# A decoder layer with 32 experts on one core: how the first expert is gathered and multiplied, where the selection stands, and the last output chunk in halves

## The chip, the core and the metric

The kernel runs on one core of one Trainium2 chip. The metric is device time in microseconds, the median of the runs; lower is better. The core has five engines with a queue each, worked off in order: TensorE (PE; its weight loads are shown apart, as PEld), VectorE (DVE), ScalarE (ACT), GpSimd (POOL) and SyncE (SP), which here does nothing but issue transfers.

## What is computed

One layer for 256 tokens of width 2048, all in float32:

```
h = rms_norm(x); proj = h @ w_in                     # 2048 x 6144
mixed = concat(moba_attention(...), diff_attention(...))
x = x + mixed @ w_out                                # 2048 x 2048
h = rms_norm(x)
group  = top-1 of 4 by  h @ w_rg + b_rg              # softmax gives g_p
expert = top-2 of 8 in the group by  h @ w_re + b_re # softmax, renormalised
for each of 32 experts e:                            # every weight is read once
    act = silu(h @ w_gate[e]) * (h @ w_up[e]) * combine[:, e]
    out += act @ w_down[e]
x = rms_norm(x + out)
```

The three expert matrices have 2048 x 512 elements each, 12.6 MB per expert and 403 MB in all.

## The kernel before, in words

Up to the experts, tokens are in two tiles of 128. w_in and w_out come in pieces of 1 MB, are split into a high and a low float32r part (L222, L223) and multiplied in three passes (L228 to L230). The last `out_product` adds w_out's last quarter to `xa` in four chunks of 512 columns. After each chunk `router_chunk` transposes the new columns of `xa` (L455), copies them to `x2T` (L457, L459), multiplies them with the router weights into `pl` (L463) and takes sums of squares into `ss2` (L467). `route` makes `rstd2` from `ss2`, copies the logits to `lgT` (L486), scales `xa` to `hp` in eight ScalarE copies (L491), turns the logits around with `sel36` (L496) and works out the mask of chosen experts and `posm`, each token's place in its expert's list (L551).

The experts then run in groups of four. A token list has C = 32 places, so a group has 128 columns. `select` (L735) compares `posm` with a counter: `sel` is a 0/1 matrix. `gather` multiplies `hp` with `sel` (L623), a pair of k at a time (k counts the 16 slices of 128 of the width), and puts the result into `hT` (L625). `expert_act` streams gate and up against 32 columns of `hT` (L702) in four column blocks of TensorE side by side: two halves of gate, two of up, for each k. `silu_mul` makes the activation, `expert_down` (L720) the down product, `put` copies it to `y`, and after four experts `scatter` adds `y` to `xa` through `swT`, the transposed `sw`, selection times weight (L632, L636). The weights of the route (`route_weights`, from L561: exponentials, `gsum`, `w1`, `comb`) and the table for lists over 32 (`overflow_table`, from L580) are called after the first expert's activation.

Weights are loaded into a ring of slots of 2 MB each: five at first, ten once the memory of the first part is free. An expert takes six (gate, up and down, two pieces each), in the order gate, up, gate, up, down, down. SyncE issues them in that order (L144), and each waits until its slot's last reader is done. The first ten slots hold expert 0 and four pieces of expert 1. The eleventh load, the first that waits for an expert, takes the slot of expert 0's first gate piece; the seventh after the ten full slots takes that of expert 1's first gate piece.

A scheduler that runs a model of the timeline orders instructions per engine; those wrapped in `tc.keep_in_program_order` keep their order among themselves. On the chip each engine works its list off in order, so an instruction that waits holds up all behind it.

Of the kernel before, what the change touches and what calls it, by code (L numbers as in the profile page):

```python
# [50 lines left out]
def hybrid_trunk_kernel(ctx: ExitStack, tc: tile.TileContext, x, norm_mix_w, w_in, lambda_q1, lambda_k1,  # L51
# [164 lines left out]

    def product(pts, lh, ll, piece, first, last, step=2):
        for k0 in range(0, 4, step):
            whl = wt("w8", [P, 2, step, CH], F32R)
            wh, wl = whl[:, 0], whl[:, 1]  # L220
            w = piece[:, k0:k0 + step, :]
            nc.scalar.activation(wh, w, AF.Copy)  # L222
            nc.vector.tensor_tensor(wl, w, wh.bitcast(F32), op=ALU.subtract)  # L223
# [173 lines left out]
    def out_product(mx, ft0, done=None):  # L397
        for dc in range(NDC):
            pts = [ps("A", [P, CH]) for _ in range(NTT)]
            piece = load_w(w_out, ft0, dc * CH)  # L400
            product(pts, lambda kt, t: mx[:, 0, kt, t * P:(t + 1) * P],
                    lambda kt, t: mx[:, 1, kt, t * P:(t + 1) * P], piece, True, True)
            for t in range(NTT):
                xs = xa[:, t, dc * CH:(dc + 1) * CH]
                nc.vector.tensor_add(xs, xs, pts[t])
            if done is not None:
                done(dc)
# [33 lines left out]
    ss2 = ct([P, NTT, NDC + 1], "ss2")  # L441
    nc.gpsimd.memset(ss2, EPS)
    pl = [None]
    lgT = wt("lgT", [P, T], bufs=1)
    nc.gpsimd.memset(lgT, 0.0)

    def router_chunk(dc):
        if dc == 0:
            pl[0] = ps("B", [P, T])
        for kp in range(2 * dc, 2 * dc + 2):  # L450
# [7 lines left out]
            if dc < NDC - 1 or kp == 2 * dc + 1:  # L458
                nc.vector.tensor_copy(x2T[:, 1, :], pt[:, 1, :])  # L459
            else:  # L460
                nc.scalar.activation(x2T[:, 1, :], pt[:, 1, :], AF.Copy)
            for k in range(2):
                nc.tensor.matmul(pl[0][64 * k:64 * k + 36, :], wrs[:, 2 * kp + k, :], x2T[:, k, :],  # L463
                                 start=kp == 0, stop=kp == NK // 2 - 1)
        for t in range(NTT):
            junk = wt("junk", [P, CH], BF16, bufs=1)
            nc.scalar.activation(junk, xa[:, t, dc * CH:(dc + 1) * CH], AF.Square, scale=D ** -0.5,  # L467
                                 accum_out=ss2[:, t, dc:dc + 1])
# [12 lines left out]
    def route():  # L481
# [3 lines left out]
        for k in range(2):  # L485
            nc.scalar.activation(lgT[64 * k:64 * k + 36, :], pl[0][64 * k:64 * k + 36, :], AF.Copy)  # L486
# [7 lines left out]
        pg = ps("B", [P, NTT, 36])  # L494
        for t in range(NTT):
            nc.tensor.matmul(pg[:, t, :], lgT[:, t * P:(t + 1) * P], sel36, start=True, stop=True)  # L496
# [53 lines left out]
        nc.tensor.matmul(pp[:, 1, :], before, m_of[1], start=False, stop=True)  # L550
        nc.vector.scalar_tensor_tensor(posm, pp, 1.0, mask.rearrange("p a g e -> p a (g e)"),  # L551
# [3 lines left out]
    def route_weights(ex, oh1, oh2, ohg):  # L555
# [7 lines left out]
        nc.vector.tensor_reduce(gsum, ex[:, :, 0, :], axis=AX.X, op=ALU.add)  # L563
# [50 lines left out]
    def gather(sel):  # L614

        hT = wt("hT", [P, NK, P], bufs=1)

        def pair(g, order=lambda i: i):
            k2 = slice(2 * g, 2 * g + 2)
            pt = ps("B", [P, 2, P])  # L620
            for k in range(2):
                for t in range(NTT):
                    order(nc.tensor.matmul(pt[:, k, :], hp[t][:, 2 * g + k, :], sel[:, t, :],  # L623
                                           start=t == 0, stop=t == NTT - 1))
            nc.vector.tensor_tensor(hT[:, k2, :], pt, bc(nfp[:, k2], [P, 2, P]), op=ALU.mult)  # L625

        return hT, pair
# [33 lines left out]
    def gu_view(w, e):  # L661
        return w[e].rearrange("(p k) f -> p k f", k=NK)
# [9 lines left out]
    def load_expert(e, n=8):  # L672


        if e not in begun:
            steps = [(i, gu_view(w, e)[:, 8 * q:8 * q + 8, :]) for q in range(2)
                     for i, w in enumerate((w_gate, w_up))]
# [13 lines left out]
    def expert_act(hT, j, weights, pair=None, order=lambda i: i, after=None, by2=True):  # L691
# [21 lines left out]
        return silu_mul(pt[:, :, 0:2, :], pt[:, :, 2:4, :], [P, 2, 2, C])  # L713

# [27 lines left out]
    def expert_group(first_e, after_first=None, last=None):  # L742
# [5 lines left out]
        for j in range(EB):  # L748
# [4 lines left out]
            if first_e + j == 0:  # L753
                act = expert_act(hT, j, w, pair, tc.keep_in_program_order)
# [242 lines left out]
```

## Time and profile before

| | |
|---|---|
| median of 3 runs | 1368.11 us (1368.02 to 1368.72) |
| the profiled execution | 1368.51 us, span 1367.0 us |
| busy share of the span | PE 78%, DVE 32%, ACT 21%, POOL 2% |
| chain that ended last | DMA 61%, PE 36%, ACT 1%, DVE 1% |
| moved | 475.52 MB, mean 348 GB/s |
| GB/s in slices 9 to 15 of 40 | 162 181 271 253 134 428 427 |

A slice is 34.2 us. The rate shows where the kernel changes its bound: about 160 to 270 GB/s while TensorE works on the attention, a hole in the thirteenth slice, then 425 to 428 GB/s to the end. PE's busy share of 78% is a mean over both parts.

### The profile page before, as it was taken

The numbers are of one execution on the slowest core, as the hardware profiler recorded it, in microseconds if no ns is written. First come the engines' busy times: TensorE is split into PE (matmuls) and PEld (weight loads), VectorE is DVE, ScalarE is ACT, GpSimd is POOL, SyncE is SP. The second block draws the span as 40 slices with busy tenths as digits, with TensorE's granted clock in tenths as the row PEclk, the third lists the DMA queues.
The fourth block names the chain that finished last, engine by engine and source line by source line (L and its number), as shares of the span: only waits on it lengthen the run. The fifth ranks groups of instructions, "written<-read, shape, count | busy, mean of one in ns | idle before, by whom it ended". The sixth has DMA issues, their size and how long they took to land.

```text
span 1367.0 us, 18082 instructions
## 1 busy us (share of the span) xinstructions
PE 1065.1 (78%) x7821; PEld 637.9 (47%) x7821; DVE 435.1 (32%) x863; ACT 292.0 (21%) x510; POOL 28.3 (2%) x34
## 2 busy tenths in 40 slices
PE   8999999999998859568765956775585685667775
PEld 6888888888875424224322422432242242224232
DVE  5565674554563313102201310211131031113123
ACT  5545444444443100000000000000000000000103
POOL 1000000010000000000000000000000000000000
PEclk9999999999999979867978977888898798689888
DMA  9954555555663999999999999999999999999994
GB/s 337 315 187 155 159 173 177 169 162 181 271 253 134 428 427 427 428 426 426 428 427 427 428 428 426 426 428 428 428 426 427 428 427 427 427 427 425 426 419 147
DMA packets 70545, 475.52 MB, mean 348 GB/s; under 512 B 8983, under 2 KB 9533, under 8 KB 46141
## 3 DMA queue, kind: packets, MB, share of 16 engines
q1 hardware_dynamic: 70384, 474.30, 85.3%
q8 instruction: 63, 1.03, 0.3%
q14 instruction: 20, 0.16, 0.0%
q10 hardware_dynamic: 78, 0.03, 0.0%
HBM read 472.21 MB, written 2.10 MB: 347 GB/s over the span
## 4 chain that ended last, share of the span: by engine, by line
DMA 61%; PE 36%; ACT 1%; issue 1%; DVE 1%; SPq 0%; DVEq 0%; ACTq 0%
DMA slot<-in_w_up_dram 37%; DMA slot<-in_w_down_dram 17%; PE psA L229 9%; PE psA L228 9%; PE psA L230 9%; DMA slot<-in_w_gate_dram 6%; PE psB L702 3%; PE psB L720 1%; PE psB L623 1%; ACT hp L491 1%; PE psA L645 1%; PE psB L309 1%; PE psB L463 1%; PE psB L304 0%; DMA xa<-in_x_dram 0%
## 5 line engine op out<-in xcount | busy, mean ns | idle before, releaser
L702 PE MATMUL psB<-slot,hT 128*32 128x256 f32 x4096 | 340.5, 473 | 176.4 <-DMA slot<-in_w_up_dram 152.2
L702 PEld LDWEIGHTS psB<-slot,hT 128*32 128x32 f32 x4096 | 158.2, 135 | 365.1 <-DMA slot<-in_w_up_dram 173.4
L720 PE MATMUL psB<-slot,act 128*32 128x512 f32 x992 | 143.4, 723 | 70.8 <-issue 51.6
L223 DVE TENSOR_TENSOR w<-slot,w 128x1024 fp32r<-128x1024 f32 (+1 forms) x130 | 157.4, 1211 | 128.1 <-ACT w L222 128.0
L222 ACT ACTIVATE w<-slot 128x1024 fp32r<-128x1024 f32 (+1 forms) x130 | 135.9, 1046 | 146.4 <-PE psA L230 128.9
L229 PE MATMUL psA<-w,xT 128*128 128x512 f32 x384 | 154.4, 402 | 0.1
L230 PE MATMUL psA<-w,xT 128*128 128x512 f32 x384 | 151.3, 395 | 0.0
L654 DVE TENSOR_SCALAR sig<-sig 128x128 f32<-128x128 f32 x32 | 7.2, 225 | 433.9 <-ACT sig L653 433.9
L228 PE MATMUL psA<-w,xT 128*128 128x512 f32 x384 | 138.2, 400 | 0.0
L708 ACT ACTIVATE gu<-psB 128x256 f32<-128x256 f32 x32 | 12.3, 384 | 577.2 <-PE psB L702 577.2
L720 PEld LDWEIGHTS psB<-slot,act 128*32 128x32 f32 x992 | 36.3, 127 | 145.5 <-issue 124.1
L728 DVE COPY y<-psB 32x512 f32<-32x512 f32 x62 | 42.7, 689 | 156.8 <-ACT y L730 156.6
L730 ACT ACTIVATE y<-psB 32x512 f32<-32x512 f32 x62 | 36.4, 588 | 242.6 <-PE psB L720 219.4
L623 PEld LDWEIGHTS psB<-sel,hp 128*128 128x128 f32 x512 | 67.9, 207 | 37.3 <-issue 22.0
L623 PE MATMUL psB<-sel,hp 128*128 128x128 f32 x512 | 74.9, 298 | 9.0 <-DVE sel L735 4.6
L229 PEld LDWEIGHTS psA<-w,xT 128*128 128x128 f32 x384 | 72.1, 188 | 18.4 <-DVE w L223 1.5
L230 PEld LDWEIGHTS psA<-w,xT 128*128 128x128 f32 x384 | 72.1, 188 | 16.6
L228 PEld LDWEIGHTS psA<-w,xT 128*128 128x128 f32 x384 | 70.6, 188 | 15.8
L645 PE MATMUL psA<-y,swT 128*128 128x512 f32 x128 | 61.7, 604 | 3.5 <-ACT y L730 3.5
L625 DVE TENSOR_TENSOR hT<-psB,nfp 128x256 f32<-128x256 f32 x64 | 27.2, 424 | 80.6 <-PE psB L623 80.4
L229 PE MATMUL psA<-w,mx 128*128 128x512 f32 x128 | 52.4, 409 | 0.0
L648 DVE TENSOR_TENSOR xa<-xa,psA 128x512 f32<-128x512 f32 x64 | 43.6, 687 | 24.6 <-PE psA L645 24.4
(250 smaller groups left out, 710.3 us busy)
## 6 DMA issues: line engine op xcount, KB each, us to landing
slot<-in_w_gate_dram SPq DMA_DIRECT2D x64, 2048.0 KB, 39.1
slot<-in_w_up_dram SPq DMA_DIRECT2D x64, 2048.0 KB, 33.1
slot<-in_w_down_dram SPq DMA_DIRECT2D x62, 2048.0 KB, 38.4
slot<-in_w_in_dram SPq DMA_DIRECT2D x47, 1024.0 KB, 5.3
slot<-in_w_out_dram SPq DMA_DIRECT2D x16, 1024.0 KB, 5.0
slot<-in_w_down_dram SPq DMA_DIRECT2D x4, 1024.0 KB, 25.0
out_dram<-xa SPq DMA_DIRECT2D x8, 256.0 KB, 3.5
xa<-in_x_dram SPq DMA_DIRECT2D x3, 512.0 KB, 5.8
```

The source lines that it names most:

```text
L222: nc.scalar.activation(wh, w, AF.Copy)
L223: nc.vector.tensor_tensor(wl, w, wh.bitcast(F32), op=ALU.subtract)
L228: nc.tensor.matmul(pts[t], lh(kt, t), wh[:, k, :], start=st, stop=False)
L229: nc.tensor.matmul(pts[t], lh(kt, t), wl[:, k, :], start=False, stop=False)
L230: nc.tensor.matmul(pts[t], ll(kt, t), wh[:, k, :], start=False, stop=sp)
L623: order(nc.tensor.matmul(pt[:, k, :], hp[t][:, 2 * g + k, :], sel[:, t, :], start=t == 0, stop=t == NTT - 1))
L645: nc.tensor.matmul(po, swT[:, t * P:(t + 1) * P], y[:, dc * CH:(dc + 1) * CH], start=True, stop=True)
L648: nc.vector.tensor_add(xs, xs, po)
L702: order(nc.tensor.matmul(pgu[q:q + C, :], hT[:, k, j * C:(j + 1) * C], w[k // 8][:, k % 8, h * H:(h + 1) * H], start=k == 0, stop=k == NK ...
L720: nc.tensor.matmul(py[32 * dc:32 * dc + C, :], act[:, f % 2, f // 2, :], d[f // 2][:, f % 2, dc * CH:(dc + 1) * CH], start=f == 0, stop=f ...
L728: nc.vector.tensor_copy(dst, py[32 * dc:32 * dc + C, :])
L730: nc.scalar.activation(dst, py[32 * dc:32 * dc + C, :], AF.Copy)
```

## The change

In the last chunk of the last `out_product` both splits of w_out are made first, and the product runs in two halves of 256 columns, each with its own additions to `xa` and its own call of `router_chunk`. The router's first six pairs go through `lgT` and `sel36` as before, but right after the sixth; the last two are multiplied the other way round, straight into the logits. Six warming matmuls follow the matmuls for `posm`. The reduce for `gsum` is pinned to the program's order. Expert 0 loads gate, gate, up, up, has a function of its own (`first_act`), and gathers only its own 32 columns; expert 1 gathers the other 96. Cut to its core:

```diff
+    def split(w):
+        whl = wt("w8", [P, 2, w.shape[1], CH], F32R)
+        ...
     def out_product(mx, ft0, done=None):
...
+            if done is None or dc < NDC - 1:
...
+            parts = [split(piece[:, k0:k0 + 2, :]) for k0 in (0, 2)]
+            H = CH // 2
+            for hf in range(2):
+                cols = slice(hf * H, (hf + 1) * H)
+                for kt in range(4):
+                    wh, wl = (w[:, kt % 2, cols] for w in parts[kt // 2])
+                    for t in range(NTT):
+                        tk = slice(t * P, (t + 1) * P)
+                        for i, (a, b) in enumerate(((lh, wh), (lh, wl), (ll, wh))):
+                            nc.tensor.matmul(pts[t][:, cols], a[kt][:, tk], b,
+                                             start=kt == 0 and i == 0, stop=kt == 3 and i == 2)
+                for t in range(NTT):
+                    xs = xa[:, t, dc * CH + hf * H:dc * CH + (hf + 1) * H]
+                    nc.vector.tensor_add(xs, xs, pts[t][:, cols])
+                done(2 * dc + hf, 1)
     def router_chunk(kp0, n):
...
+                if kp < EARLY:
+                    nc.tensor.matmul(pl[0][64 * k:64 * k + 36, :], wrs[:, 2 * kp + k, :], x2T[:, k, :], ...
+                    continue
+                for t in range(NTT):
+                    nc.tensor.matmul(pl[1][:, t, :], x2T[:, k, t * P:(t + 1) * P], wrs[:, 2 * kp + k, :], ...
+            if kp == EARLY - 1:
+                for k in range(2):
+                    nc.scalar.activation(lgT[64 * k:64 * k + 36, :], pl[0][64 * k:64 * k + 36, :], AF.Copy)
+                pl[1] = ps("B", [P, NTT, 36])
+                for t in range(NTT):
+                    nc.tensor.matmul(pl[1][:, t, :], lgT[:, t * P:(t + 1) * P], sel36, start=t == 0, ...
     def route():
...
+        keep_warm(6, ident, ident)
     def route_weights(ex, oh1, oh2, ohg):
...
-        nc.vector.tensor_reduce(gsum, ex[:, :, 0, :], axis=AX.X, op=ALU.add)
+        tc.keep_in_program_order(nc.vector.tensor_reduce(gsum, ex[:, :, 0, :], axis=AX.X, op=ALU.add))
     def load_expert(e, n=8):
...
+            if e > 0:
+                steps[1], steps[2] = steps[2], steps[1]
...
+    def first_act(hT, weights, pair):
+        pin = tc.keep_in_program_order
+        pgu = ps("B", [P, 2, P])
+        for i, w in enumerate(weights[:2]):
+            for k in range(NK):
+                if i == 0 and k % 2 == 0:
+                    for g in {0: (0, 1), 2: (), 4: (2, 3), NK - 2: ()}.get(k, (k // 2 + 1,)):
+                        pair(g, pin, 0, C)
+                for c in range(4):
+                    h, par = c // 2, c % 2
+                    pin(nc.tensor.matmul(pgu[32 * c:32 * c + C, i, :], hT[:, k, 0:C],
+                                         w[k // 8][:, k % 8, h * T:(h + 1) * T].rearrange(
+                                             "p (j c) -> p c j", c=2)[:, par, :],
+                                         start=k == 0, stop=k == NK - 1))
...
             if first_e + j == 0:
-                act = expert_act(hT, j, w, pair, tc.keep_in_program_order)
+                act = first_act(hT, w, pair)
+            elif first_e + j == 1:
+                act = expert_act(hT, j, w, lambda g, order: pair(g, order, C, P))
```

Three places in the engines' lists. First VectorE around the first selection (`sel`; `r_ex` holds the exponentials, `r_gsum` and `r_w` belong to the weights). Before:

```order
L551 SCALAR_TENSOR_TENSOR posm<-psB_3221,mask 128x64 [waits DVE_49,PE_49]
L563 TENSOR_REDUCE r_gsum_3367<-r_ex_3194 128x2 [waits Activation_49]
L565 TENSOR_SCALAR r_w_473_3369<-r_ex_3194 128x8
L735 TENSOR_TENSOR sel_3231<-iota_118,posm 128x256 [waits DVE_49]
L735 TENSOR_TENSOR sel_3772<-iota_118,posm 128x256
L566 TENSOR_TENSOR r_w_473_3369<-r_w_473_3369,r_gsum_3367 128x8 [waits DVE_49]
```

Changed:

```order
L583 SCALAR_TENSOR_TENSOR posm<-psB_3255,mask 128x64 [waits DVE_49,PE_49]
L597 TENSOR_SCALAR r_w_476_3474<-r_ex_3228 128x8 [waits Activation_49]
L793 TENSOR_TENSOR sel_3272<-iota_118,posm 128x256 [waits DVE_49]
L793 TENSOR_TENSOR sel_3925<-iota_118,posm 128x256
L657 TENSOR_TENSOR hT_3274<-psB_3283,nfp 128x2x32 [waits PE_49]
```

The reduce of `r_gsum` has moved behind; `r_w`, with a wait for ScalarE, stands between `posm` and the selection.

Second, VectorE from the first activation (`act`) to the scatter weights (`sw`; `o_cum`, `o_fe`, `item_e` and `nitem` are the overflow table's, `hit` in the code is `y` here). Before:

```order
L658 TENSOR_TENSOR act_3363<-act_3363,psB_3356 128x128 [waits DVE_49]
L598 COPY o_cum_3395<-psB_3393 128x64 [waits PE_49]
L632 TENSOR_TENSOR sw_3408<-sel_3231,comb 128x256
L602 TENSOR_TENSOR y_3397<-o_cum_3395,iota_118 128x512 [waits DVE_49]
L607 CAST nitem<-o_cum_3395 1x1
```

Changed, the twelve rows that end with `sw` (ahead of them, behind `act`: `r_gsum`, two of `r_w`, `o_cum` and the first `y`):

```order
L639 CAST nitem<-o_cum_3500 1x1
L600 TENSOR_TENSOR r_w_476_3474<-r_w_476_3474,r_ohg_3248 128x8 [waits DVE_49]
L636 TENSOR_REDUCE o_fe_3504<-y_3502 128x16 [waits DVE_49]
L601 TENSOR_TENSOR r_w_477_3475<-r_w_476_3474,r_ex_3228 128x8 [waits DVE_49]
L602 TENSOR_TENSOR comb<-r_oh_450_3233,r_w_476_3474 128x64
L637 TENSOR_SCALAR o_fe_3504<-o_fe_3504 128x16 [waits DVE_49]
L640 TENSOR_TENSOR y_3502<-y_3502,o_cum_3500 128x512
L603 TENSOR_TENSOR r_oh_453_3243<-r_oh_453_3243,r_w_477_3475 128x64 [waits DVE_49]
L638 CAST item_e<-o_fe_3504 1x16 [waits DVE_49]
L604 TENSOR_TENSOR comb<-comb,r_oh_453_3243 128x64 [waits DVE_49]
L641 TENSOR_REDUCE o_fe_3504<-y_3502 128x16 [waits DVE_49]
L664 TENSOR_TENSOR sw_3513<-sel_3272,comb 128x256 [waits DVE_49]
```

`sw` has moved from the second instruction behind `act` to the seventeenth.

Third, TensorE where expert 1 begins (L636 and L668 transpose `sw`, L720 and L778 are expert 0's down product, `slot_3136` and `slot_3175` expert 1's first gate piece). Before:

```order
L636 MATMUL psB_3410<-ident,sw_3408 128x128 [waits DVE_49,PE_49]
L636 MATMUL psB_3410<-ident,sw_3408 128x128
L720 MATMUL psB_3415<-slot_105,act_3363 32x512 [waits DMAHW0_49]
L720 MATMUL psB_3415<-slot_105,act_3363 32x512 x7
L720 MATMUL psB_3415<-slot_3135,act_3363 32x512 [waits DMAHW1_49]
L720 MATMUL psB_3415<-slot_3135,act_3363 32x512 x7
L702 MATMUL psB_3442<-slot_3136,hT_3233 32x256 [waits DMAHW2_49,PE_49]
```

Changed:

```order
L778 MATMUL psB_3520<-slot_3174,act_3468 32x512 [waits DMAHW1_49]
L778 MATMUL psB_3520<-slot_3174,act_3468 32x512 x7
L655 MATMUL psB_3548<-sel_3272,hp_3196 128x96 [waits PE_49]
L655 MATMUL psB_3548<-sel_3272,hp_3197 128x96
L655 MATMUL psB_3548<-sel_3272,hp_3196 128x96
L655 MATMUL psB_3548<-sel_3272,hp_3197 128x96
L655 MATMUL psB_3554<-sel_3272,hp_3196 128x96
L655 MATMUL psB_3554<-sel_3272,hp_3197 128x96
L655 MATMUL psB_3554<-sel_3272,hp_3196 128x96
L655 MATMUL psB_3554<-sel_3272,hp_3197 128x96
L736 MATMUL psB_3547<-slot_3175,hT_3274 32x256 [waits DMAHW2_49,DVE_49,Activation_49]
```

Two pairs of the gather (four matmuls each) stand ahead of expert 1's first k; four more pairs follow between its first gate and its first up matmuls, and the last two behind its eighth k.

## Rows read from the trace of the kernel before

**Rows 1.** Windows: span, busy time per engine, granted clock, DMA share, GB/s
```profile
430.00:431.00 1.00, 0.14 (x1) 0.17 (x2) 0.85 (x5) 0.12 (x2) 0.00 (x0) 0.81 0.00 0
...
600.00:1200.00 600.00, 407.65 (x3678) 187.90 (x3682) 111.15 (x211) 38.47 (x86) 0.00 (x0) 0.82 1.01 427
```

**Rows 2.** Timeline of SyncE's queue: start us, us, engine, line, operation, tile
```profile
422.20 0.33 SPq L144 DMA_DIRECT2D slot<-in_w_up_dram  x1
441.36 0.80 SPq L144 DMA_DIRECT2D slot<-in_w_down_dram  x2
...
457.15 0.33 SPq L144 DMA_DIRECT2D slot<-in_w_gate_dram  x1
...
462.78 0.80 SPq L144 DMA_DIRECT2D slot<-in_w_down_dram  x2
```

**Rows 3.** Chain of waits, first expert: start us, us, what
```profile
430.86 3.54 PE psB L623 x16
...
436.26 1.98 PE psB L623 x16
...
439.25 1.09 PE psB L623 x8
440.33 1.00 PE psB L702 x16
...
446.60 1.93 PE psB L702 x32
...
453.52 5.77 PE psB L720 x32
459.29 6.99 PE psB L702 x128
```

**Rows 4.** Timeline of TensorE, last chunk to the route's mask; columns as rows 2
```profile
406.88 0.71 PE L228 MATMUL psA<-w,mx 128*128 128x512 f32 x2
...
421.49 0.64 PE L496 MATMUL psB<-sel,lgT 128*128 128x36 f32 x4 [0.92 <-ACT lgT L486]
421.96 4.26 PE L181 MATMUL psB<-ident 128*128 128x128 f32 x36
...
426.11 0.18 PE L550 MATMUL psB<-mask,before 128*128 128x32 bf16 x1
```

**Rows 5.** Timeline of VectorE: rstd2, the selection, scatter weights and overflow table
```profile
417.06 0.16 DVE L483 TENSOR_REDUCE var<-ss 128x2 f32<-128x10 f32 x1 [0.51 <-ACT junk L467]
...
419.47 0.42 DVE L459 COPY qkT<-psB 128x256 f32<-128x256 f32 x1 [1.49 <-ACT qkT L457]
...
420.64 0.28 DVE L141 TENSOR_TENSOR rstd<-rstd,rsq_cu 128x1 f32<-128x1 f32 x2
...
430.15 0.16 DVE L563 TENSOR_REDUCE r_gsum<-r_ex 128x2 f32<-128x8 f32 x1 [3.60 <-ACT r_ex L561]
...
452.30 0.41 DVE L632 TENSOR_TENSOR sw<-sel,comb 128x256 f32<-128x256 f32 x1
452.63 0.68 DVE L602 TENSOR_TENSOR y<-o_cum,iota 128x512 f32<-128x512 f32 x1
...
455.43 0.69 DVE L609 TENSOR_REDUCE o_fe<-y 128x16 f32<-128x512 f32 x1
```

**Rows 6.** Timeline of ScalarE: last square, logits, hp copies
```profile
416.30 0.63 ACT L467 ACTIVATE junk<-xa 128x512 bf16<-128x512 f32 x1 [0.86 <-DVE xa L405]
...
420.67 0.77 ACT L486 ACTIVATE lgT<-psB 36x256 f32<-36x256 f32 x2 [1.23 <-PE psB L463]
421.46 8.55 ACT L491 ACTIVATE hp<-xa,rstd 128x512 f32<-128x512 f32 x8
```

**Rows 7.** Chain of waits, last output chunks; columns as rows 3
```profile
400.42 0.23 PE psA L229
...
410.84 0.55 PE psB L463 x2
```

**Rows 8.** Groups by form: line, operation, tiles, shape, count, busy us, mean ns
```profile
L230 PEld LDWEIGHTS psA<-w,mx 128*128 128x128 f32 x128 | 24.0, 188 | 5.2
```

More of the change, by code (lines that the diff above doesn't have):

```diff
@@ L215, in load_w @@
         return piece
+    def split(w):
+        whl = wt("w8", [P, 2, w.shape[1], CH], F32R)
+        wh, wl = whl[:, 0], whl[:, 1]
+        nc.scalar.activation(wh, w, AF.Copy)
+        nc.vector.tensor_tensor(wl, w, wh.bitcast(F32), op=ALU.subtract)
+        return wh, wl
     def product(pts, lh, ll, piece, first, last, step=2):
         for k0 in range(0, 4, step):
[L219 to L223, printed above, removed]
+            wh, wl = split(piece[:, k0:k0 + step, :])
             for k in range(step):
@@ L400, in out_product @@
             piece = load_w(w_out, ft0, dc * CH)
[L401 to L407, printed above, removed]
+            lh, ll = ([mx[:, i, kt, :] for kt in range(4)] for i in range(2))
+            if done is None or dc < NDC - 1:
+                product(pts, lambda kt, t: lh[kt][:, t * P:(t + 1) * P],
+                        lambda kt, t: ll[kt][:, t * P:(t + 1) * P], piece, True, True)
+                for t in range(NTT):
+                    xs = xa[:, t, dc * CH:(dc + 1) * CH]
+                    nc.vector.tensor_add(xs, xs, pts[t])
+                if done is not None:
+                    done(2 * dc, 2)
+                continue
[14 more added lines that the diff above has]
+                done(2 * dc + hf, 1)
     wrs = wt("wrs", [P, NK, 36], bufs=1)
@@ L439, in router_consts, with router_chunk @@
                                 base=0, channel_multiplier=-1)
-    ss2 = ct([P, NTT, NDC + 1], "ss2")
+    ss2 = ct([P, NTT, NDC + 2], "ss2")
     nc.gpsimd.memset(ss2, EPS)
-    pl = [None]
     lgT = wt("lgT", [P, T], bufs=1)
     nc.gpsimd.memset(lgT, 0.0)
-    def router_chunk(dc):
-        if dc == 0:
+    pl = [None, None]
+    EARLY = 6
+    def router_chunk(kp0, n):
+        if kp0 == 0:
             pl[0] = ps("B", [P, T])
-        for kp in range(2 * dc, 2 * dc + 2):
+        for kp in range(kp0, kp0 + n):
             pt = ps("B", [P, 2, T])
@@ L484, in route @@
         rsqrt1([(rstd2[:, t:t + 1], v[:, t:t + 1]) for t in range(NTT)], "rsq_c")
-        for k in range(2):
-            nc.scalar.activation(lgT[64 * k:64 * k + 36, :], pl[0][64 * k:64 * k + 36, :], AF.Copy)
         for t in range(NTT):
@@ L493, in route @@
                                      AF.Copy, scale=rstd2[:, t:t + 1])
-        pg = ps("B", [P, NTT, 36])
-        for t in range(NTT):
-            nc.tensor.matmul(pg[:, t, :], lgT[:, t * P:(t + 1) * P], sel36, start=True, stop=True)
+        pg = pl[1]
         keep_warm(18, ident, ident)
@@ L675, in load_expert @@
         if e not in begun:
-            steps = [(i, gu_view(w, e)[:, 8 * q:8 * q + 8, :]) for q in range(2)
-                     for i, w in enumerate((w_gate, w_up))]
+            steps = [(i, gu_view(w, e)[:, 8 * q:8 * q + 8, :]) for i, w in enumerate((w_gate, w_up))
+                     for q in range(2)]
+            if e > 0:
+                steps[1], steps[2] = steps[2], steps[1]
             if e < NE - 1:
@@ L713, in expert_act @@
         return silu_mul(pt[:, :, 0:2, :], pt[:, :, 2:4, :], [P, 2, 2, C])
+    def first_act(hT, weights, pair):
[12 more added lines that the diff above has]
+                                         start=k == 0, stop=k == NK - 1))
+        gu = wt("gu", [P, 2 * P])
+        nc.scalar.activation(gu, pgu.rearrange("p a b -> p (a b)"), AF.Copy)
+        pt = ps("B", [P, 2, 2, 2, C])
+        for i in range(2):
+            nc.tensor.transpose(pt[:, i].rearrange("p a b s -> p (a b s)"), gu[:, i * P:(i + 1) * P], ident)
+        a, u = (pt[:, i].rearrange("p h c s -> p c h s") for i in range(2))
+        return silu_mul(a, u, [P, 2, 2, C])
     def expert_down(act, weights):
```

31 lines of the change are left out of this document (18 added, 13 removed).

## The prediction

> **What bounds the kernel now.** I read the page's slices and its chain of waits first. The reader is to see two regimes: up to about 420 us TensorE works without a pause, and from about 441 to 1330 us the queue of expert weights never stops. The windows give its rate, 427 GB/s between 600 and 1200, and show a hole: nothing moves between 430 and 431 [rows 1]. So the end of the kernel is the moment at which the stream restarts for good, plus a fixed number of bytes. One slot is 2.097 MB, at 427 GB/s 4.91 us. If the n-th load after the hole (n from 0) can be issued at time t, the stream behaves as if it had restarted at t − 4.91 n; the largest of these decides, and a microsecond there is a microsecond of the kernel.
>
> The second view is SyncE's queue [rows 2]. The tenth slot is requested at 422.20 and lands by about 427; load 0 follows at 441.36, when the first expert has read the first gate piece through its eighth k. That is the binding release. Load 4 (457.15) counts as 437.5 and load 6 (462.78) as 433.3: early by 4 and by 8 us. These are reserves that a change can eat.
>
> The third view, the chain in order of time, gives the first expert [rows 3]: gather of two pairs in 3.54 us, two more pairs in 1.98, one pair in 1.09, two k of matmuls in 1.00. The first group is slow because the granted clock fell to its lower level in the slice from 430 to 431 (mean 0.81) [rows 1], after TensorE had stood idle since 426.3 [rows 4]. What it waited for is the selection: the first instruction of the weights on VectorE, gsum, starts at 430.15, released by the exponential on ScalarE [rows 5], which stands behind eight hp copies of 8.55 us [rows 6].
>
> **Part 1, last output chunk by halves, and the router.** 24 matmuls of 512 columns become 48 of 256. At 512 one takes 0.23 us [rows 7]. The nearest rows for one full weight load per matmul at fewer columns: 36 and 128 columns both run at 0.118 us a record (0.47 us from the first of 4 to the next group, 4.26 for 36) [rows 4]. Half of 0.23 is about the same, so I take 0.12; the other end is 0.188, the length of one such weight load by its own record [rows 8], which would add 3.3 us over 48. To the chunk's start, 406.9 [rows 4], I add 48 × 0.12 = 5.8, eight transposes at 0.12 = 1.0 and seven router steps of 0.55 [rows 7] = 3.85: 417.5. The same sum for the chunk of before falls 0.3 short of its trace, so 417.8. The two lgT copies, 0.77 us, were the last step before; now they stand on ScalarE ahead of the last square of ss2. They end at 418.6, the square (half of 0.63, and its read) at 419.1 [rows 6]. From the reduce to rstd2 VectorE took 417.06 to 420.92, of which 1.5 us were a wait for a router copy [rows 5]; without that wait, but with two copies of 0.42 woven in, rstd2 is there at 422.0. The hp copies start then, against 421.46: 0.5 later. The logits lose the lgT copy and L496 from their path, but wait for rstd2 instead: no gain.
>
> **Part 2, selection and warming.** In the changed order gsum is gone from ahead of the selection, but w1, which reads the same exponentials and waits for ScalarE, still stands there. So the wait stays: 422.0 + 8.55 (hp) + 0.2 (exponential) + 0.2 (w1) + 0.5 (selection to first gather): 431.4, against 430.86. The six warming matmuls (12 records of 0.118 us) end near 427.7 and TensorE still stands idle for 3.7 us, before for 4.6. I take the same fall of the clock; without it 1.6 us (3.54 against 1.98) would be saved.
>
> **Part 3, the first expert.** 32 gather columns in place of 128: since the 36-column row costs as much as the 128-column one [rows 4], the 64 records go from 9.9 us to about 9.5 and no lower. [...]
>
> Gate and up were 32 steps of 256 columns, four column blocks side by side, two k (four steps) in 1.00 us. Now they are 64 steps of 128 columns, with twice the weight loads and every second element of the moving operand. Bounds: 0.115 (columns alone) to 0.23 us (nothing won by the shorter row); I take 0.12, near the 128-column row. [...] In all the expert takes 17.4 us against 17.7 and ends at 448.8 (before 448.53 [rows 3]). The first gate piece is free after five pairs (3.54 + 1.98 + 1.09, less 0.3) and eight k of the gate alone (1.9): 439.6, so load 0 goes at 439.7. Alone that is a gain of 1.7 us. Load 1, at about 444.6, just keeps up.
>
> **Part 4, what was pushed behind.** The route's weights now run on VectorE after the first activation, woven into the overflow table, and the scatter weights sw stand behind both. Before, sw started at 452.30, ahead of the table, which ran from 452.63 to 456.12 [rows 5]. Less two instructions of 0.33 us that moved away the table is 2.8 us, and the seven small instructions of the weights (gsum 0.16) add about 0.6: sw comes 3.4 us later in its chain. TensorE's transposes of sw stand ahead of the first down product, so that starts at 448.8 + (453.52 − 448.53) + 3.4 = 457.2. It lasts 5.8 us as before, at a low clock again [rows 3]: 463.0, against 459.29. Then expert 1 gathers the other 96 columns: six of its eight pairs stand ahead of its eighth k, 48 records at 0.12, with turns 6.0 us, on top of 3.49 us for eight k (459.29 to 462.78 [rows 2, 3]). Its first piece is free at 472.5. That is load 6: 472.5 − 29.5 = 443.0, against 441.36. Load 4, after half the down product (about 460.5), counts as 440.9. So the reserve of 8 us is eaten, and the binding release moves from load 0 to load 6.
>
> **Sum.** +0.5 (tail) − 0.2 (first expert) + 3.4 (sw) + 6.0 (gather) − 8.0 (reserve) = +1.7 us, all on the path, since the stream runs dry for some 3 us before load 6. The profiled execution took 1368.51 us (span 1367.0), 0.4 over the median of the runs, 1368.11. On the median the forecast is **1369.8 us**.
>
> **Rivals.**
> (a) The first release decides. Expert 1 would be on time after all, so that the 1.7 us of load 0 stand: 1366.4. For: in my sum load 6 alone is late, by 3.3 us. Against: sw and gather are in-order work with a row for each length.
> (b) Slower than can be mistaken for no change. The place is the 64 short steps of the first expert: bound by weight loads and not by columns, a step costs up to 0.23 us, 64 × 0.11 = +7 us ahead of load 6, 1376.8. It decides from 0.136 us a step, where the loss passes 2.7 us. For: twice the loads for the same columns. Against: 128-column records at 0.118. The same mechanism in the 256-column halves (0.188) gives +3.3: 1373.1.
> (c) The change does what its words say, and the selection follows posm. The gather then starts when the warming ends, 427.7, 3.7 us earlier, and the clock may stay up (1.6): load 6 counts as 439.3 to 437.7, −2.1 to −3.7 us, 1366.0 to 1364.4. Against: w1 and its wait stand ahead. That this part does nothing is thus in my forecast.
>
> **Chances.** Forecast 0.47, (a) 0.15, (b) 0.30, (c) 0.08. About 0.2%, 2.7 us, is what a measurement of this kernel can tell from no change. Same: 0.42 of the forecast, 0.12 of (a), 0.05 between them and the others, 0.59; slower: 0.28 of (b) and 0.05 of the forecast's upper edge, 0.33; faster: 0.08 from (c) and (a). The likeliest case alone spans 1368.3 to 1371.5 (0.6 us on the tail, 1 us on the clock). The range takes in (a), most of (c) and most of (b): 1366.0 to 1375.5.
>
> **What would show it.** Right: load 0 issued 1 to 2 us before 441.36, the selection on VectorE still right after the exponential near 431, sw near 456, load 6 near 472 with the transfers dry before it. Wrong: the selection near 427, half steps well over 0.13 us, or load 6 before 469.

## The result and the profile after

The changed kernel took **1379.65 us** (1376.90 to 1382.93, 4 runs), the kernel before 1368.41 us beside it: ratio 1.0079 [1.0067, 1.0092], 11.2 us slower. The forecast was 1369.8 us with a range to 1375.5: outside it. The profiled execution took 1382.93 us (span 1381.4). Its last output chunk starts 4.5 us later than before (411.42 against 406.88 in [rows 4]), in code that the change doesn't touch; in a second profile of the same kernel it was 1.4 us, and over the traces of this document it starts between 406.67 and 411.42. Moments are therefore compared from that chunk's start.

TensorE's timeline of the changed kernel, from the last chunk to the second expert (start us, us, engine, line, operation, tiles, shape, count, idle time before and its releaser):

```profile
411.42 1.65 PE L423 MATMUL psA<-w,mx 128*128 128x256 f32 x12
412.91 0.60 PE L479 MATMUL psB<-ident,xa 128*128 128x128 f32 x4
...
431.73 1.58 PE L181 MATMUL psB<-ident 128*128 128x128 f32 x12
436.46 2.02 PE L655 MATMUL psB<-sel,hp 128*128 128x32 f32 x16 [3.14 <-DVE sel L793]
438.41 1.94 PE L761 MATMUL psB<-slot,hT 128*32 128x128 f32 x32
440.27 3.62 PE L655 MATMUL psB<-sel,hp 128*128 128x32 f32 x16
443.83 1.08 PE L761 MATMUL psB<-slot,hT 128*32 128x128 f32 x16
444.84 1.92 PE L655 MATMUL psB<-sel,hp 128*128 128x32 f32 x8
...
455.27 6.38 PE L761 MATMUL psB<-slot,hT 128*32 128x128 f32 x160
...
469.21 0.66 PE L668 MATMUL psB<-ident,sw 128*128 128x128 f32 x2 [4.24 <-DVE o_fe L642]
469.80 4.86 PE L778 MATMUL psB<-slot,act 128*32 128x512 f32 x32
474.60 2.02 PE L655 MATMUL psB<-sel,hp 128*128 128x96 f32 x16
```

A count is of records; a float32 matmul shows as two (the six warming matmuls as 12). Read the groups of 32-column products (L655) downwards: the first 16 records take 2.02 us, the next 16 take 3.62, then each 8 take 1.92. Sixteen records of the gate's steps (L761), four steps, take 1.08; in the run with w1 held back, below, 0.66. The first expert lasts from 436.46 to 461.65, 25.2 us; in [rows 3] it lasted 17.7. Why, the windows of the same trace say (span; busy time of PE, PEld, DVE, ACT, POOL; granted clock; DMA share; GB/s):

```profile
436.00:437.00 1.00, 0.54 (x5) 0.57 (x6) 0.65 (x2) 0.00 (x0) 0.00 (x0) 1.00 0.00 0
438.00:439.00 1.00, 1.00 (x16) 0.89 (x19) 0.23 (x1) 0.00 (x0) 0.00 (x0) 0.59 0.00 0
440.00:442.00 2.00, 2.00 (x16) 1.73 (x9) 0.00 (x0) 0.00 (x0) 0.00 (x0) 0.50 0.00 0
458.00:459.00 1.00, 1.00 (x32) 0.92 (x28) 0.00 (x0) 0.00 (x0) 0.00 (x0) 0.67 1.22 246
```

The granted clock falls in the slice from 438 to 439 (mean 0.59), from 1.00 to 0.50, and is back only in that from 458 to 459 (0.67), some 3 us after the gather's last group. The first group still ran at 1.00 (436 to 438): the fall came 2 us into the gather, not in the idle stretch ahead of it (1.00 from 434 to 436). Before, the fall of [rows 1] (0.50 from 432 to 434) was over by the second group of [rows 3] (1.98 us; 0.99 from 434 to 436, then 1.00).

VectorE of the changed kernel (columns as above), the selection and the scatter weights, to be laid beside [rows 5]:

```profile
435.81 0.17 DVE L597 TENSOR_SCALAR r_w<-r_ex 128x8 f32<-128x8 f32 x1 [3.67 <-ACT r_ex L593]
435.89 0.75 DVE L793 TENSOR_TENSOR sel<-iota,posm 128x256 f32<-128x256 f32 x2
...
468.65 0.41 DVE L664 TENSOR_TENSOR sw<-sel,comb 128x256 f32<-128x256 f32 x1
```

w1 (L597) waits 3.67 us for the exponential and the selection stands behind it, as forecast. SyncE's queue, beside [rows 2]:

```profile
447.83 9.76 SPq L144 DMA_DIRECT2D slot<-in_w_down_dram  x2
...
473.02 0.33 SPq L144 DMA_DIRECT2D slot<-in_w_gate_dram  x1
...
484.17 0.80 SPq L144 DMA_DIRECT2D slot<-in_w_down_dram  x2
```

Load 6 goes at 484.17 and counts as 484.17 − 29.5 = 454.7, against 441.36 for the release that bound before: 13.3 us, of which 4.5 are the late chunk and 8.8 the change. The transfers show the same loss in one row. Windows from 440 to 500 of the kernel before, of the changed one, and of the fastest version below (columns as above; the last is GB/s):

```profile
440.00:500.00 60.00, 44.50 (x539) 22.29 (x538) 15.69 (x40) 5.90 (x13) 0.00 (x0) 0.89 0.97 405
```
```profile
440.00:500.00 60.00, 50.49 (x579) 35.00 (x575) 15.13 (x51) 3.61 (x9) 0.00 (x0) 0.76 0.78 312
```
```profile
440.00:500.00 60.00, 43.23 (x600) 22.00 (x596) 13.99 (x36) 5.89 (x13) 0.00 (x0) 0.88 1.01 423
```

At 427 GB/s the changed kernel loses (427 − 312) / 427 × 60 = 16.2 us of the stream in this stretch, the kernel before 3.1; the difference is 13.1 us, beside the 13.3 of load 6.

### The profile page after: what moved, and what is told of

Read it like the earlier page. It is cut to its first block, busy times and chain, and to the rows that moved or that the text cites. A ratio compares the mean times of both kernels' runs of the same rounds, so it can differ in the third digit from the quotient of the medians.

```text
span 1381.4 us, 18566 instructions
## 1 busy us (share of the span) xinstructions
PE 1090.3 (79%) x8057; PEld 661.5 (48%) x8057; DVE 435.5 (32%) x874; ACT 292.0 (21%) x513; POOL 28.6 (2%) x34
## 5 line engine op out<-in xcount | busy, mean ns | idle before, releaser
L736 PE MATMUL psB<-slot,hT 128*32 128x256 f32 x3968 | 327.0, 466 | 165.2 <-DMA slot<-in_w_up_dram 145.6
L736 PEld LDWEIGHTS psB<-slot,hT 128*32 128x32 f32 x3968 | 153.3, 133 | 344.9 <-DMA slot<-in_w_up_dram 163.9
L778 PE MATMUL psB<-slot,act 128*32 128x512 f32 x992 | 155.0, 775 | 70.3 <-issue 51.6
L778 PEld LDWEIGHTS psB<-slot,act 128*32 128x32 f32 x992 | 38.9, 134 | 153.2 <-issue 132.2
L655 PEld LDWEIGHTS psB<-sel,hp 128*128 128x128 f32 x576 | 79.4, 211 | 43.1 <-issue 34.5
L655 PE MATMUL psB<-sel,hp 128*128 128x128 f32 (+2 forms) x576 | 87.6, 301 | 6.7 <-DVE sel L793 5.2
L657 DVE TENSOR_TENSOR hT<-psB,nfp 128x256 f32<-128x256 f32 (+2 forms) x72 | 28.4, 394 | 98.9 <-PE psB L655 98.8
L232 PE MATMUL psA<-w,mx 128*128 128x512 f32 x120 | 49.1, 409 | 0.0
```

The lines of the kernel that those rows point to most:

```text
L736: order(nc.tensor.matmul(pgu[q:q + C, :], hT[:, k, j * C:(j + 1) * C], w[k // 8][:, k % 8, h * H:(h + 1) * H], start=k == 0, stop=k == NK ...
L778: nc.tensor.matmul(py[32 * dc:32 * dc + C, :], act[:, f % 2, f // 2, :], d[f // 2][:, f % 2, dc * CH:(dc + 1) * CH], start=f == 0, stop=f ...
```

## The experiments

The theories, as the expectations name them: **N**, the narrow gather (32 columns) keeps the clock down; **S**, the short steps (128 columns) do; **I**, the idle stretch between warming and gather brings it down. Later **T**: narrow gather and short steps together bring it down by themselves.

**Wide gather in the first expert.**

```diff
-                        pair(g, pin, 0, C)
+                        pair(g, pin)
```

> The changed kernel, but expert 0 gathers all 128 columns (expert 1 gathers its 96 again, as in the change). Theory N: the 32-column gather keeps the granted clock at its lower level (in the changed kernel from 438 to 459 us, 25.2 us for expert 0's matmuls). With the wide gather the clock should rise after the first pairs as in the kernel before, expert 0 take about 17.5 us, and load 6 come 7.5 us earlier: 1372 us (1370 to 1374). Rival S: the short steps of 128 columns keep the clock down or cost too much by themselves: expert 0 still 24 to 25 us, about 1379.5 us.

1374.55 us (1370.71 to 1377.37), ratio 1.0025 [1.0012, 1.0038]. Half-way between the two theories: the clock falls here too (0.97 from 434 to 436, 0.50 from 436 to 438), but comes back before the second group of short steps (0.68, then 1.00 from 440 to 442), and the first expert takes 19.0 us (434.45 to 453.5). TensorE's timeline, and the window in which the clock rises:

```profile
434.45 2.46 PE L655 MATMUL psB<-sel,hp 128*128 128x128 f32 x16 [3.15 <-DVE sel L793]
436.83 1.94 PE L761 MATMUL psB<-slot,hT 128*32 128x128 f32 x32
438.70 2.32 PE L655 MATMUL psB<-sel,hp 128*128 128x128 f32 x16
440.95 0.66 PE L761 MATMUL psB<-slot,hT 128*32 128x128 f32 x16
```
```profile
438.00:440.00 2.00, 2.00 (x25) 1.60 (x18) 0.00 (x0) 0.00 (x0) 0.00 (x0) 0.68 0.00 0
```

Four times the columns in the same number of records, and in this execution the clock is back some 3 us after its fall; with 32 it stayed down for 20.

**Narrow gather with the old steps and the old order of loads.**

```diff
-            if e > 0:
-                steps[1], steps[2] = steps[2], steps[1]
+            steps[1], steps[2] = steps[2], steps[1]
...
-                act = first_act(hT, w, pair)
+                act = expert_act(hT, j, w, lambda g, order: pair(g, order, 0, C), tc.keep_in_program_order)
```

> The changed kernel with the 32-column gather, but expert 0 streams gate and up together in steps of 256 columns and loads gate, up, gate, up as before. Theory N: the granted clock still stays at its lower level for most of expert 0, 23 to 25 us of matmuls, load 6 still binds: 1379 us (1376 to 1382). Rival S: with the old steps the clock rises, expert 0 takes 17.5 us: 1372 us.

1370.97 us (1369.27 to 1373.09, and one at 1386.03; 10 runs), ratio 1.0022 [0.9997, 1.0047]: near the 1372 of S, so my theory N was wrong. TensorE's timeline:

```profile
432.42 3.60 PE L655 MATMUL psB<-sel,hp 128*128 128x32 f32 x16 [3.13 <-DVE sel L792]
435.94 3.24 PE L735 MATMUL psB<-slot,hT 128*32 128x256 f32 x32
439.11 1.97 PE L655 MATMUL psB<-sel,hp 128*128 128x32 f32 x16
```

The clock is down for the first group and most of the first steps (0.50 from 432 to 438, 0.84 from 438 to 440), and back in the second group (1.97 us; 1.00 from 440 to 442), behind the first 256-column steps. With only one of the two edits the clock came back within the first expert, in some 3 us (wide gather) and some 7 (old steps); with both it stayed down for 20.

**w1 held behind gsum,** so that the selection follows the slot positions.

```diff
-        nc.vector.tensor_scalar(w1, ex[:, :, 1, :], 1.0, None, op0=ALU.add)
+        tc.keep_in_program_order(nc.vector.tensor_scalar(w1, ex[:, :, 1, :], 1.0, None, op0=ALU.add))
```

> The changed kernel with w1 pinned behind gsum, so that the selection follows posm. Theory N: the selection comes some 3.5 us earlier, the gather starts at the end of the warming matmuls, but the clock still falls in the narrow gather and stays down: 1376 us (1374 to 1378). Rival I: it was the idle stretch between warming and gather that brought the clock down; without it the clock stays up through expert 0 and the kernel takes 1369 us (3.5 and 7.5 less).

1367.62 us (1366.10 to 1373.36, 10 runs), ratio 0.9991 [0.9979, 1.0004]: 12 us under the changed kernel, from the place of one instruction, and on the side of rival I. TensorE's timeline and a window:

```profile
426.98 1.58 PE L181 MATMUL psB<-ident 128*128 128x128 f32 x12
428.40 1.87 PE L655 MATMUL psB<-sel,hp 128*128 128x32 f32 x16
430.20 1.12 PE L761 MATMUL psB<-slot,hT 128*32 128x128 f32 x32
431.25 1.97 PE L655 MATMUL psB<-sel,hp 128*128 128x32 f32 x16
433.16 0.66 PE L761 MATMUL psB<-slot,hT 128*32 128x128 f32 x16
...
439.56 4.10 PE L761 MATMUL psB<-slot,hT 128*32 128x128 f32 x130
```
```profile
434.00:436.00 2.00, 2.00 (x30) 1.75 (x29) 0.23 (x1) 0.00 (x0) 0.00 (x0) 1.00 0.00 0
```

The gather follows the warming without a gap; the same narrow gather and short steps run at 1.00 throughout, and the first expert takes 16.7 us (428.40 to 445.1). That is 8.5 us less than with the fall; the gather also starts 3.3 us earlier (21.73 us after the chunk, at 406.67, against 25.04).

**The version that I expected to be best:** before, with gsum and w1 pinned and called behind the fifth pair of the first expert, gate whole and then up in short steps, one wide gather, no halves.

```diff
-        nc.vector.tensor_scalar(w1, ex[:, :, 1, :], 1.0, None, op0=ALU.add)
+        tc.keep_in_program_order(nc.vector.tensor_scalar(w1, ex[:, :, 1, :], 1.0, None, op0=ALU.add))
...
-                act = expert_act(hT, j, w, pair, tc.keep_in_program_order)
+                act = first_act(hT, w, pair, lambda: route_weights(*routed))
...
-        route_weights(*routed)
```

> The kernel before with three things: selection right behind posm (the weights on VectorE behind the fifth pair of expert 0), gate whole and then up in short steps, and the wide gather in expert 0; no halves, no second gather in expert 1. Theory N: the clock stays up, the first gate piece is free about 434.3 us against 441.4, load 1 and load 0 bind together near 434.5: 1361.5 us (1360 to 1364). Rival S: the short steps bring the clock down; expert 0 takes 22 us or more and load 0 comes no earlier than 438: 1365 us or more.

**1363.73 us** (1362.54 to 1365.04, 4 runs), ratio 0.9952 [0.9935, 0.9968]: inside the range of N, and 0.5% under the kernel before. Its row above shows why, a stream at 423 GB/s from 440 on; the clock stays at 1.00 through its gather and steps (windows from 420 to 442 and from 444 to 448).

**The idle stretch filled, selection unchanged.**

```diff
-        keep_warm(6, ident, ident)
+        keep_warm(18, ident, ident)
```

> The changed kernel with 18 warming products instead of 6 between the slot positions and the selection, so that TensorE has work through the 3.14 us in which it waited for the selection; the selection, the gather and the steps are unchanged. I (the idle stretch brings the granted clock down, and the thin work after it only fails to raise it): the clock stays at 1.00 in the gather and the steps, the first expert takes some 17 us instead of 25.2, and the time is 1379.65 - 8.4 = 1371.2 us. T (the 32-column gather beside the short steps brings the clock down by itself, whatever stands ahead of it): the clock falls some microseconds into the gather, and the time stays at 1379 to 1380 us.

1371.45 us (1368.93 to 1381.91, 12 runs), ratio 1.0021 [1.0005, 1.0036], just what I gives. But the profiled execution was one of three above 1375 us (1376.72), and in it the clock fell as T has it. TensorE's timeline and a window:

```profile
427.19 4.26 PE L181 MATMUL psB<-ident 128*128 128x128 f32 x36
431.95 1.94 PE L655 MATMUL psB<-sel,hp 128*128 128x32 f32 x16 [0.49 <-DVE sel L793]
433.82 1.55 PE L761 MATMUL psB<-slot,hT 128*32 128x128 f32 x32
435.30 3.62 PE L655 MATMUL psB<-sel,hp 128*128 128x32 f32 x16
```
```profile
434.00:436.00 2.00, 2.00 (x36) 1.61 (x28) 0.15 (x1) 0.00 (x0) 0.00 (x0) 0.58 0.04 8
```

With 0.49 us of idle time the clock still fell, some 2 us after the gather began, and stayed down past the end of the gather at 450.3: it read 0.50 to 454 and a mean of 0.76 from 450 to 460, which puts its return near 455. So the fall does not need an idle stretch of 3 us. That it is rarer without one is read from the times alone: nine of these twelve executions lie under 1374 us, and none of the changed kernel's.

**The second expert gathers nothing** (the first one wide).

```diff
-            elif first_e + j == 1:
-                act = expert_act(hT, j, w, lambda g, order: pair(g, order, C, P))
```

> The changed kernel in which the first expert gathers all 128 columns and the second expert gathers nothing (the run with the wide gather, less the second expert's own gather). Theory: the second expert's gather stands on the path, 6.08 us between its start and load 6 more than before: 1374.55 - 6.1 = 1368.5 us. Rival: loads 4 and 5 and the queue behind them cover it, so the time stays near 1374 us.

1371.14 us (1368.99 to 1373.75, 11 runs), ratio 1.0009 [1.0000, 1.0018]: 3.4 us less than with the second gather, not 6.1. I had forgotten what is late next: load 4. SyncE's queue of the run with the second gather (loads 4 and 6), and of this one (load 4):

```profile
465.40 0.33 SPq L144 DMA_DIRECT2D slot<-in_w_gate_dram  x1
...
477.25 0.80 SPq L144 DMA_DIRECT2D slot<-in_w_down_dram  x2
```
```profile
464.92 0.33 SPq L144 DMA_DIRECT2D slot<-in_w_gate_dram  x1
```

They count as 477.25 − 29.5 = 447.8 and 464.92 − 19.6 = 445.3, from chunks at 409.40 and 410.40: 3.5 us apart. Not all of this is the gather. In the run that has it, load 4 counts as 465.40 − 19.6 = 445.8, 2.0 us ahead of load 6, and that is what the gather alone could give there; the other 1.5 us belong to these two executions, since the clock fell in that one and not in this (first expert 19.0 and 17.9 us). Two windows of this run speak against I:

```profile
434.00:436.00 2.00, 0.58 (x5) 0.61 (x6) 0.83 (x3) 0.74 (x2) 0.00 (x0) 1.00 0.00 0
436.00:438.00 2.00, 2.00 (x33) 1.68 (x35) 0.85 (x2) 0.00 (x0) 0.00 (x0) 1.00 0.00 0
```

TensorE had idled 3.13 us before this gather, and the clock did not fall (1.00 from 434 to 446). In the run with the second gather it fell (0.50 from 436 to 438) behind 3.15 us of idle time, in the same groups of matmuls. So idle time of this length does not bring the fall in every execution.

**Halves and router alone,** the kernel before with `out_product` and the router of the change.

```diff
...
-                done(dc)
...
+                done(2 * dc + hf, 1)
```

> The kernel before with only the last output chunk by halves and the router's early sum (lgT ahead, two column blocks), nothing else. By the trace of the change its tail from the chunk's start to the gather is 1.06 us longer: 1368.4 + 1.1 = 1369.5 us, same chain of the first expert as before. Rival H (the halves do save what they are built for, and the 1.06 us belongs to the selection's place behind the weights): 1367.9 us or less, gather earlier than 23.98 us after the chunk's start.

1371.21 us (1369.65 to 1374.09, 12 runs), ratio 1.0012 [1.0003, 1.0022]: 1.8 us slower, and rival H falls. The gather starts 25.08 us after the chunk (407.87 to 432.95), against 23.98 before: 1.1 us as expected, and the interval (0.4 to 3.0 us) holds that. ScalarE, and a window:

```profile
423.54 8.57 ACT L524 ACTIVATE hp<-xa,rstd 128x512 f32<-128x512 f32 x8 [1.03 <-DVE rstd L141]
432.01 0.20 ACT L592 ACTIVATE r_ex<-r_ex 128x16 f32<-128x16 f32 x1
```
```profile
438.00:440.00 2.00, 2.00 (x26) 0.96 (x19) 0.00 (x0) 0.00 (x0) 0.00 (x0) 0.73 0.03 8
```

The halves bring nothing, because the selection waits for the exponential behind the hp copies, and these for rstd2, not for the logits: they start 15.67 us after the chunk, against 14.58 in [rows 6]. Load 0 goes 2.5 us later than before, not 1.1, because the clock stayed down longer in this execution: it fell in the slice from 432 to 434 (0.56), read 0.50 to 438 and came back between 438 and 440 (0.73), some 7 us for some 3 before, with the same gather and the same steps.

**Weights called early in the changed kernel** (gsum and w1 pinned, the chain behind the fifth pair).

```diff
...
+                if i == 0 and k == 7:
+                    weights_now()
...
-        route_weights(*routed)
```

> The changed kernel with the expert weights' chain (gsum and w1 first) held back until the fifth pair of the first expert's gather has been copied, and called there, not after the first expert: the selection follows the slot positions at once, as in the run with w1 behind gsum, and the slot weights sw are ready before the first expert ends. I: no idle ahead of the gather, clock at 1.00, first expert 16.7 us as there; and without the 3.2 us that the late sw cost the down projection: 1367.6 - 3.2 = 1364.4 us. Rival: the weights' own instructions on VectorE, standing between the gather's copies, hold the later pairs up by as much as they save (about 3 us): 1367 to 1368 us.

1369.62 us (1365.04 to 1372.73, 11 runs), ratio 0.9999 [0.9990, 1.0009]: no gain over the run with w1 pinned, where I expected 3.2 us. Not for the rival's reason: TensorE can transpose sw 42.6 us after the chunk's start against 46.3 there, so 3.6 us were won. The stream shows a part of them:

```profile
440.00:500.00 60.00, 50.19 (x682) 30.94 (x681) 17.35 (x46) 5.91 (x13) 0.00 (x0) 0.91 0.99 415
```

From 440 it runs at 415 GB/s, against 402 in the run with w1 pinned. That would be about 1.8 us gained; the median is 2 us higher instead. In the profiled executions the time from load 6 to the end of the span is 4.1 us longer than with w1 pinned, and 2.8 of these lie behind the last weight load (35.7 us against 32.9). Why stays open; the two runs were also on different chips.

**The changed kernel once more.**

> The changed kernel unaltered, for a second profile and more times. In the run with more warming the clock fell in the profiled execution although TensorE did not idle, and in the run without the second expert's gather it did not fall although TensorE idled 3.13 us; so the question is whether the fall belongs to the kernel or to the execution. K (idle and thin work together bring it down in nearly every execution): first expert again near 25 us, times 1376 to 1383. X (it depends on the execution): some executions near 1371 us, in which the first expert takes 17 us.

1380.97 us (1377.53 to 1383.90, 6 runs), ratio 1.0084 [1.0071, 1.0097]. K holds: the clock falls again, and the first expert takes 26.8 us (433.37 to 460.1).

```profile
434.00:436.00 2.00, 2.00 (x15) 1.94 (x14) 0.23 (x1) 0.00 (x0) 0.00 (x0) 0.59 0.00 0
```

All ten executions of this kernel lie at 1376.9 us or more.

**Idle stretch filled and wide gather,** both edits together.

> The changed kernel with both: 18 warming products, so that TensorE does not idle, and the first expert gathering 128 columns (the second gathers its 96 again). If the 32-column gather is what still brought the clock down in some executions of the run with more warming (1375 to 1382 us in 3 of 12), then here no execution is above 1374 us, and the median is 1370 to 1371 us. If the narrow gather has nothing to do with it, some executions are again above 1375 us.

1373.30 us (1371.37 to 1377.49, 7 runs), ratio 1.0029 [1.0018, 1.0040]. The expectation fell: three executions lie above 1374 us. In the profiled one, 1377.49 us, gather and steps run at 1.00 and the first expert takes 16.7 us, but the clock had fallen earlier, beside the 36-column products of the router (0.66 from 422 to 424, 0.50 from 424 to 428, 0.64 from 428 to 430):

```profile
420.31 0.64 PE L496 MATMUL psB<-sel,lgT 128*128 128x36 f32 x4 [0.92 <-ACT lgT L493]
...
421.89 3.13 PE L489 MATMUL psB<-wrs,qkT 128*128 128x36 f32 x16
424.82 6.47 PE L181 MATMUL psB<-ident 128*128 128x128 f32 x36
```

The 16 records of the router took 2.05 us in the run with only the idle stretch filled, and the 36 of warming 4.26; the gather starts 27.7 us after the chunk here, against 25.1 there. So an execution above 1375 us is by itself no sign of a fall in the gather.

**Selection first, alone,** in the kernel before.

```diff
...
-                act = expert_act(hT, j, w, pair, tc.keep_in_program_order)
+                act = expert_act(hT, j, w, pair, tc.keep_in_program_order,
+                                 lambda q: route_weights(*routed) if q == 1 else None)
...
-        route_weights(*routed)
```

> The kernel before with the selection alone moved ahead: gsum and w1 held back until the first expert's gate and up have begun, no halves, no own gather, the old steps. Load 0 then goes out about 5 us earlier: 1369.4 - 5 = 1364.4 us, beside 1363.7 us of the version that takes the gate whole, then up in short steps as well. Rival: the selection is no gain without the short steps, since load 1 still waits for all of gate and up: 1367 us or more.

1365.14 us (1362.66 to 1366.24, 6 runs), ratio 0.9966 [0.9954, 0.9977]: 0.7 us from what I expected, and the rival (1367 or more) falls. TensorE's timeline and SyncE's queue:

```profile
427.76 2.02 PE L623 MATMUL psB<-sel,hp 128*128 128x128 f32 x16 [0.94 <-DVE sel L735]
```
```profile
436.74 0.80 SPq L144 DMA_DIRECT2D slot<-in_w_down_dram  x2
```

The gather starts 20.34 us after the chunk (at 407.42), 3.6 earlier than before, and its first group takes 2.02 us for 3.54; the windows from 430 to 446 read 1.00. Load 0 goes at 436.74, 4.6 us before [rows 2]. So 4.1 us of the 5.5 that the fastest version gains come with the selection's place alone; the two intervals overlap, so the 1.4 us between them are not shown to be the short steps' gain.

**Own gathers in the fastest version** (32 columns in the first expert, 96 in the second).

> The version that was faster than both kernels (selection first, gate whole then up in short steps, one wide gather, no halves), with the first expert gathering its own 32 columns and the second its 96. If the second gather costs on the path what the run without it showed, 1374.55 - 1371.14 = 3.4 us: 1363.7 + 3.4 = 1367.1 us. Rival: with the loads early the second gather lies beside transfers that run without a break, and costs under 1 us: 1364 to 1364.5 us.

1365.94 us (12 runs), ratio 0.9983 [0.9963, 1.0003], but in two groups: seven from 1360.74 to 1366.68 and five from 1370.15 to 1373.55. The profiled execution (1363.88) is of the first: its gather's first group takes 1.94 us, and the clock reads 1.00 in the windows from 430, inside that gather, to 446; there the second gather costs nothing, as the rival had it: load 6 counts as 28.2 us after the chunk, the deciding load of the fastest version as 28.6. Whether the second group is the fall of the clock was not seen. The fastest version's four runs, with its wide gather, lie within 2.5 us.

## Why the prediction was wrong, point by point

**The step that failed: "I take the same fall of the clock", and with it the 17.4 us of Part 3.** I saw the fall in [rows 1], saw TensorE idle 3.7 us in the new order (3.14 in the trace), and priced the fall at what it had cost before, 1.6 us. What followed it was no longer the same work: beside narrow gather and short steps together the clock stayed at 0.50 for some 20 us. The first expert took 25.2 us in place of 17.4; these 7.8 us are more than the whole miss by load 6, 8.8 − 1.7 = 7.1. That it is the clock and not the new work itself, the run with w1 behind gsum shows: the same gather and steps take 16.7 us at 1.00. So the fall cost 8.5 us here, not 1.6. Why the clock stays down beside this work stays open. That load 6 decides and load 0 does not was forecast rightly, though load 0 went 1.9 us later after the chunk, not 1.7 earlier. The other steps, in the profile's sum:

- Tail: +1.1 for +0.5; the half products at 1.49 / 12 = 0.124 us (from 411.42 to 412.91) for 0.12.
- Selection behind w1 and the exponential: as forecast.
- Short steps: with w1 held back, 130 records in 4.10 us, four to a step, 0.126 us for 0.12. Steps bound by their loads, rival (b), are thereby ruled out, and every second element of the moving operand cost nothing that shows. That the 1376.8 us of (b) came near the measured time is luck.
- sw: down starts 8.15 us after the first expert's end for 4.99 before, +3.2 for +3.4.
- Gather in the second expert: 474.60 to 484.17 is 9.57 us for 3.49, +6.1 for +6.0. Down itself was 1.0 shorter.
- Sum: 1.1 + 7.5 + 3.2 − 1.0 + 6.1 − 8.1 = 8.8 us. The second profile, in which the clock fell within the gather's first group and the first expert took 26.8 us, gives 10.9 by load 6 (483.19 − 29.5, chunk at 408.32); the medians say 11.2 and 11.7. Where the 2.4 us between 8.8 and 11.2 lie is not shown: the four executions differ by 6 us among themselves.

The rule that a load n counts as its time less 4.91 n, and the latest decides, held. For each run the load that decides by it, how much later than before that is (both from the last chunk's start, 34.5 us before), and the measured median against that of before in the same comparison:

| run | deciding load | by the rule, us | median, us |
|---|---|---|---|
| changed kernel | 6 | +8.8 | +11.2 |
| the same once more | 6 | +10.9 | +11.7 |
| wide gather | 6 | +3.9 | +5.3 |
| old steps | 6 | +3.0 | +1.8 |
| w1 behind gsum | 6 | −1.9 | −1.6 |
| weights early | 6 | −3.9 | +0.2 |
| idle filled | 6 | +9.2 | +2.0 (this execution +7.3) |
| idle filled, wide gather | 6 | +5.5 | +4.0 |
| no second gather | 4 | +0.4 | +1.7 |
| halves alone | 0 | +2.5 | +1.8 |
| selection alone | 0 | −5.2 | −4.1 |
| fastest version | 1 | −5.9 | −5.5 |
| the same, own gathers | 6 | −6.3 | −3.3 (this execution −5.4) |

All but the weights early agree within some 2.5 us, or with the execution that was profiled. The rule's figure comes from one execution and the median from all, so some of this is chance: the profiled executions of the wide gather and of idle filled with wide gather, for two, lay 8.2 us above before's median. The traces by themselves are the better check. From the moment at which the deciding load says that the stream restarted (its time less 4.91 n) to the end of the span it is 925.6 us before, 926.7 in the changed kernel, 924.6 to 928.3 in eleven others, and 929.2 with the weights early.

Rival (c), the selection after the slot positions at 1366.0 to 1364.4, was built as the run with w1 behind gsum: 1367.62, 1.6 us under the kernel before in its comparison, where (c) had 2.1 to 3.7. The clock stayed up (1.00 from 420 to 442), and load 6 still decided.

## What to carry to other kernels

When an edit makes TensorE's work thinner (fewer columns, the same number of instructions) right behind an idle stretch, ask not only whether the clock falls there but for how long, and price the whole stretch at the lower level as a bound (here 0.50 for some 20 us, 8.5 us of the first expert). Read from the changed order what stands ahead of the instruction that the gather waits for: here one leftover instruction of 0.17 us held the selection back, and moving it was worth 12 us in the changed kernel. Try the parts of a change one by one: selection first was worth 4.1 us, the halves with their router cost 1.8, and the narrow gather saved the first expert 0.7 us (427.20 to 443.24 against 427.40 to 444.1) that no median shows.

## What the runs showed of the hardware

- The gather's columns cost next to nothing at either level: 16 records of 32 columns took 1.97 us at a granted clock of 1.00 (w1 behind gsum) and 3.62 at 0.50 (changed kernel), of 128 columns 2.05 at 1.00 (no second gather) and 3.75 at 0.50 (halves alone).
- How long the clock stayed at 0.50 after a fall, by the windows: some 3 us in the kernel before (0.81 from 430 to 431, 0.99 from 434 to 436) and with wide gather and short steps (0.97 from 434 to 436, 0.68 from 438 to 440); some 7 us with narrow gather and 256-column steps (0.95 from 430 to 432, 0.84 from 438 to 440), in halves alone (0.56 from 432 to 434, 0.73 from 438 to 440), whose gather and steps are those of before, and under the 128-column warming (0.66 from 422 to 424, 0.64 from 428 to 430); 20 to 24 us in three executions with narrow gather and short steps (changed kernel: 0.59 from 438 to 439, 0.67 from 458 to 459; the same once more: 0.59 from 434 to 436, 0.94 from 458 to 460; idle filled: 0.58 from 434 to 436, back near 455). So it is both edits together that stand apart; between 3 and 7 us the same work gave either.
- Narrow gather and short steps with less than 1 us of idle time ahead: the clock fell in one profiled execution (0.58 from 434 to 436, 0.49 us idle) and not in three others (w1 behind gsum and weights early, no idle time; own gathers in the fastest version, 0.94 us). With 3.1 us of idle time before a wide gather it fell in one (0.50 from 436 to 438, wide gather) and not in another (1.00 from 434 to 446, no second gather). What tells such executions apart was not settled; those two were also on different chips.
